# Adaptive max pooling on one core: a small load at the head of the load queue instead of a side load in its middle

## The chip, the core and the metric

The kernel runs on one core of one Trainium2 chip. The metric is the device time of one execution in microseconds (us). The kernel before was run three times: 340.25, 340.25 and 339.33 us, so its median is 340.25 us.

## What is computed

The input `x` is 32 x 256 x 4096 in float32 (134.2 MB). Each row of 4096 values is cut into 256 equal windows of 16 values, and the output holds the maximum of each window (32 x 256 x 256, 8.4 MB).

```python
for i in range(output_size):                 # 256
    start = int(i * length / output_size)    # 16 * i
    end = int((i + 1) * length / output_size)
    result[:, :, i] = np.max(x[:, :, start:end], axis=-1)
```

All windows are alike and lie one after the other in memory, so the kernel sees one long list of 2,097,152 windows of 64 bytes each and may cut it as it likes.

## The kernel before

**The cut.** The list of windows is cut into three spans that follow each other in memory. The first is the *side* span: 16 partitions with 384 windows each (24 KB a partition, L35). The remaining 2,091,008 windows are spread over 128 partitions, 16,336 to a partition, in two groups (L37): group 0 has 7,600 windows a partition, group 1 has 8,736. Within a group a partition owns one contiguous run of memory (486,400 bytes in group 0, 559,104 bytes in group 1).

**The loads.** A group is loaded in pieces of `CHUNK` = 760 windows: 128 partitions x 47.5 KB, 6,080 KB in all. I call such a piece a full load. Group 0 gives 10 of them, group 1 gives 11 and a last piece of 376 windows (23.5 KB a partition). `load` (L73 to L76) takes the next slot of the ring, issues one DMA from SyncE (the profile's SP queue) and has VectorE (DVE) reduce the slot with one `reduce_max` (L67) into an output tile that stays in SBUF.

**The ring.** `ring` (L41) has three slots of 128 x 47.5 KB, taken in turn by a counter `n_loads`. A load can be issued only when the reduce of the load three places before it has freed its slot. All DMAs, loads and stores, are issued by SP in the order in which the program has them, and a DMA whose slot isn't free holds up all that stand behind it on SP.

**The side load.** When `n_loads` is 11, that is after 10 loads of group 0 and one of group 1, `load_side` (L81 to L89) takes one slot of the ring and issues two DMAs: one for 15 partitions of 24 KB (L84), and one for the last partition (L85), whose row is written as 16 pieces of 1.5 KB. Then one reduce over 16 partitions goes into the tile `side`.

**The stores.** They stand behind all loads on SP, in this order: group 0 (128 x 30,400 bytes), the side tile (16 x 1,536 bytes, put second by L104), the first 7,600 windows of group 1 (128 x 30,400 bytes), and the last 1,136 windows of group 1 (128 x 4,544 bytes). Each waits for the reduces that fill what it stores.

Of the kernel before, what the change touches and what calls it, by code (L numbers as in the profile page):

```python
# [1 line left out]

# [4 lines left out]


@with_exitstack
def kernel(  # L10
    ctx: ExitStack,
    tc: tile.TileContext,
    x: bass.AP,
    output_size: bass.AP,
    out: bass.AP,
):

    nc = tc.nc
    P = nc.NUM_PARTITIONS
    fp32 = mybir.dt.float32

    B, C, L = x.shape
    O = int(output_size)
    assert L % O == 0, (L, O)
    W = L // O
    total = B * C * O  # L30

    SLOTS = 3
    CHUNK = 760

    SIDE_P, SIDE, SIDE_AT = 16, 384, 11  # L35
    rest = (total - SIDE_P * SIDE) // P
    GROUPS = [10 * CHUNK, rest - 10 * CHUNK]  # L37
    CUT = 10 * CHUNK

    pool = ctx.enter_context(tc.tile_pool(name="pool", bufs=1))  # L40
    ring = pool.tile([P, SLOTS, CHUNK * W], fp32, tag="ring", name="ring")  # L41

    xw = x.flatten_outer_dims().rearrange("r (o w) -> (r o) w", w=W)
    ow = out.flatten_outer_dims().rearrange("r o -> (r o)")

    taken = 0

    def group(parts, n):

        nonlocal taken  # L50
        span = slice(taken, taken + parts * n)
        taken += parts * n
        return (
            xw[span].rearrange("(p n) w -> p (n w)", p=parts),
            ow[span].rearrange("(p n) -> p n", p=parts),
        )

    n_loads = 0

    def next_slot(parts, n):  # L60
        nonlocal n_loads
        slot = ring[0:parts, n_loads % SLOTS, 0 : n * W]
        n_loads += 1
        return slot

    def pooled(dst, src):
        nc.vector.reduce_max(  # L67
            out=dst,
            in_=src.rearrange("p (n w) -> p n w", w=W),
            axis=mybir.AxisListType.X,  # L70
        )

    def load(dst, src, a, b):  # L73
        slot = next_slot(P, b - a)
        nc.sync.dma_start(out=slot, in_=src[:, a * W : b * W])  # L75
        pooled(dst[:, a:b], slot)  # L76

    xs, os_ = group(SIDE_P, SIDE)
    side_out = pool.tile([SIDE_P, SIDE], fp32, tag="side", name="side")

    def load_side():  # L81
        slot = next_slot(SIDE_P, SIDE)
        last = SIDE_P - 1
        nc.sync.dma_start(out=slot[0:last], in_=xs[0:last])  # L84
        nc.sync.dma_start(  # L85
            out=slot[last:SIDE_P].rearrange("p (k n) -> p k n", k=16),
            in_=xs[last:SIDE_P].rearrange("p (k n) -> p k n", k=16),
        )
        pooled(side_out, slot)  # L89

    stores = []
    for g, n in enumerate(GROUPS):
        xg, og = group(P, n)
        o = pool.tile([P, n], fp32, tag=f"out{g}", name=f"out{g}")
        for a in range(0, n, CHUNK):
            if n_loads == SIDE_AT:
                load_side()
            load(o, xg, a, min(a + CHUNK, n))
        for a, b in ((0, CUT), (CUT, n)):
            if a < b:  # L100
                stores.append((og[:, a:b], o[:, a:b]))
    assert taken == total

    stores.insert(1, (os_, side_out))  # L104
    for dst, src in stores:
        nc.sync.dma_start(out=dst, in_=src)


# [1 line left out]
_INS = ['x', 'output_size']  # L110
_OUTS = [((32, 256, 256), 'float32')]

_NUMBERS = {'output_size': 256}


# [26 lines left out]
```

## Time and profile before

| what | us |
|---|---|
| median of three runs | 340.25 |
| the profiled execution's own time | 340.25 |
| span of the profiled execution | 338.48 |
| around the span (340.25 - 338.48) | 1.77 |
| first load issued by SP | 0.73 |
| first reduce starts (first full load has landed) | 17.87 |
| one reduce of a full load (128 x 760 windows) | 12.82 |
| last reduce (128 x 376 windows) starts and ends | 323.65, 330.06 |
| DVE busy in all | 281.9 |

In the profile's tables an instruction is named by its line in the kernel, its engine, and the tiles that it writes and reads: `out<-ring` is a reduce, `ring<-in_x_dram` a load, `out_dram<-out` a store. DVE is VectorE, and SPq is the time of SyncE's queue of instructions, here the issue of DMAs. "DMA share" is the mean busy share of the core's 16 DMA engines; it can go over 1 where packets overlap. The trace also holds each DMA packet with its start, its duration and its size. A packet is the run of bytes of one partition, so a full load has 128 packets of 48,640 bytes, 8 to each DMA engine. The core's clock was granted in full (1.00).

### The profile page before, as it was taken

Reading aid. Unit: us, or ns where it says so; the run is one execution under the profiler, and the core shown is the slowest. Engines: PE = TensorE matmul, PEld = TensorE weight load, DVE = VectorE, ACT = ScalarE, POOL = GpSimd, SP = SyncE. Lnnn points to the kernel's source line nnn. Section 1 sums busy time; section 2 is a strip of 40 time slices with the busy share of each in tenths; the row PEclk is TensorE's granted clock in tenths of the full one; section 3 lists DMA queues with packets and bytes.
Section 4 is the critical chain, followed back from the end, with each engine's and each line's share of the span. In section 5 each row is a group of like instructions: output and inputs, shape, how many; then the busy total and the mean of one; then the engine's idle time right before and its main releaser. Section 6 shows DMA issues by size and latency. Waiting matters only on the chain.

```text
span 338.5 us, 117 instructions
## 1 busy us (share of the span) xinstructions
DVE 281.9 (83%) x23; POOL 0.2 (0%) x4
## 2 busy tenths in 40 slices
DVE  0088989889898898989799998989889898898990
POOL 0000000000000000000000000000000000000000
DMA  9999999999999999999999999999999999999995
GB/s 356 414 425 460 437 391 460 454 408 425 460 437 391 460 448 402 437 460 397 288 448 408 431 454 431 408 454 448 402 437 454 431 408 448 454 397 423 441 420 245
DMA packets 3664, 142.61 MB, mean 421 GB/s; under 512 B 432, under 2 KB 448, under 8 KB 576
## 3 DMA queue, kind: packets, MB, share of 16 engines
q1 hardware_dynamic: 3664, 142.61, 98.7%
HBM read 134.22 MB, written 8.39 MB: 421 GB/s over the span
## 4 chain that ended last, share of the span: by engine, by line
DMA 63%; DVE 30%; issue 3%; DVEq 2%; SPq 0%
DMA ring<-in_x_dram 63%; DVE out L67 28%; DVE side L67 2%; DVEq L137 2%; SPq L75 0%
## 5 line engine op out<-in xcount | busy, mean ns | idle before, releaser
L67 DVE TENSOR_REDUCE out<-ring 128x760 f32<-128x12160 f32 (+1 forms) x22 | 275.5, 12528 | 48.1 <-DMA ring<-in_x_dram 48.1
L67 DVE TENSOR_REDUCE side<-ring 16x384 f32<-16x6144 f32 x1 | 6.5, 6529 | 0.0
L123 POOL MEMSET const-uint8-127<- 128x1 uint8 x1 | 0.1, 103 | 0.0
L123 POOL MEMSET const-bfloat16-1.0<- 128x1 bf16 x1 | 0.1, 102 | 0.0
L123 POOL MEMSET const-float32-1.0<- 128x1 f32 x1 | 0.1, 99 | 0.0
L123 POOL MEMSET const-float32-0.0<- 128x1 f32 x1 | 0.1, 98 | 0.2 <-issue 0.2
## 6 DMA issues: line engine op xcount, KB each, us to landing
ring<-in_x_dram SPq DMA_DIRECT2D x21, 6080.0 KB, 30.3
out_dram<-out SPq DMA_DIRECT2D x2, 3800.0 KB, 29.3
ring<-in_x_dram SPq DMA_DIRECT2D x1, 3008.0 KB, 23.1
out_dram<-out SPq DMA_DIRECT2D x1, 568.0 KB, 7.5
ring<-in_x_dram SPq DMA_DIRECT2D x1, 360.0 KB, 20.3
ring<-in_x_dram SPq DMA_DIRECT2D x1, 24.0 KB
out_dram<-side SPq DMA_DIRECT2D x1, 24.0 KB, 31.4
```

Of the source, the lines that this page charges most:

```text
L67: nc.vector.reduce_max(out=dst, in_=src.rearrange("p (n w) -> p n w", w=W), axis=mybir.AxisListType.X,)
L123: nc = _bacc.Bacc("TRN2", target_bir_lowering=False, num_devices=1)
L137: with _tile.TileContext(nc) as tc:
```

## The change

The side span in the middle goes away. In its place the first span of the list is 16 partitions with 128 windows each (8 KB a partition, 128 KB in all). It is loaded by one DMA ahead of all others, takes the first slot of the ring and is reduced first. Its store takes the side store's place. The remaining windows are spread over 128 partitions as before, now 16,368 to a partition: group 0 is unchanged in size, group 1 has 8,768 windows a partition (561,152 bytes), so that its last piece has 408 windows (25.5 KB a partition), and the last store has 128 x 4,672 bytes. Everything else is as it was.

```diff
-    SIDE_P, SIDE, SIDE_AT = 16, 384, 11
-    rest = (total - SIDE_P * SIDE) // P
+    FIRST_P, FIRST = 16, 128
+    rest = (total - FIRST_P * FIRST) // P
     GROUPS = [10 * CHUNK, rest - 10 * CHUNK]
     CUT = 10 * CHUNK
...
-    xs, os_ = group(SIDE_P, SIDE)
-    side_out = pool.tile([SIDE_P, SIDE], fp32, tag="side", name="side")
-
-    def load_side():
-        slot = next_slot(SIDE_P, SIDE)
-        last = SIDE_P - 1
-        nc.sync.dma_start(out=slot[0:last], in_=xs[0:last])
-        nc.sync.dma_start(
-            out=slot[last:SIDE_P].rearrange("p (k n) -> p k n", k=16),
-            in_=xs[last:SIDE_P].rearrange("p (k n) -> p k n", k=16),
-        )
-        pooled(side_out, slot)
+    xf, of = group(FIRST_P, FIRST)
+    first_out = pool.tile([FIRST_P, FIRST], fp32, tag="first", name="first")
+    slot = next_slot(FIRST_P, FIRST)
+    nc.sync.dma_start(out=slot, in_=xf)
+    pooled(first_out, slot)
...
         for a in range(0, n, CHUNK):
-            if n_loads == SIDE_AT:
-                load_side()
             load(o, xg, a, min(a + CHUNK, n))
...
-    stores.insert(1, (os_, side_out))
+    stores.insert(1, (of, first_out))
```

## The prediction

> **What bounds the kernel now.** I read the page's slices first (its second part), then SP's waits, then the timeline around the side load, then windows of equal length.
>
> ```profile
> DVE  0088989889898898989799998989889898898990
> ...
> DMA  9999999999999999999999999999999999999995
> GB/s 356 414 425 460 437 391 460 454 408 425 460 437 391 460 448 402 437 460 397 288 448 408 431 454 431 408 454 448 402 437 454 431 408 448 454 397 423 441 420 245
> ```
>
> Each column is 8.46 us. DMA is at nine tenths or more in all slices but the last, while DVE has gaps everywhere: the stream of DMA bytes sets the time. The bytes a slice jump about because a packet counts where it starts, but one slice stands out: the twentieth (161 to 169 us) moved 288 GB/s although its engines count as busy. That is where the side load runs.
>
> ```profile
> SPq L137 <- DMA out_dram<-out: 7.1, 1, 7.1
> ```
>
> This line of SP's waits shows that the end also belongs to the DMAs: after issuing the last store SP waits 7.1 us for it to land. The last store is issued at 330.01 us, but its packets begin only at 333.24 us and later, each right behind its engine's packets of the store before. So the end is the end of the byte stream, not the last reduce.
>
> ```profile
> 132.91 12.82 DVE L67 TENSOR_REDUCE out<-ring 128x760 f32<-128x12160 f32 x1 [1.57 <-DMA ring<-in_x_dram]
> 145.75 0.40 SPq L84 DMA_DIRECT2D ring<-in_x_dram  x1
> 146.21 0.23 SPq L85 DMA_DIRECT2D ring<-in_x_dram  x1
> 147.28 12.82 DVE L67 TENSOR_REDUCE out<-ring 128x760 f32<-128x12160 f32 x1 [1.56 <-DMA ring<-in_x_dram]
> 160.13 135.08 SPq L75 DMA_DIRECT2D ring<-in_x_dram  x11
> 163.29 12.82 DVE L67 TENSOR_REDUCE out<-ring 128x760 f32<-128x12160 f32 x1 [3.19 <-DMA ring<-in_x_dram]
> 176.03 6.53 DVE L67 TENSOR_REDUCE side<-ring 16x384 f32<-16x6144 f32 x1
> 182.49 12.80 DVE L67 TENSOR_REDUCE out<-ring 128x760 f32<-128x12160 f32 x1
> 195.73 12.82 DVE L67 TENSOR_REDUCE out<-ring 128x760 f32<-128x12160 f32 x1 [0.45 <-DMA ring<-in_x_dram]
> 210.12 12.82 DVE L67 TENSOR_REDUCE out<-ring 128x760 f32<-128x12160 f32 x1 [1.57 <-DMA ring<-in_x_dram]
> ```
>
> A reduce that waited for a DMA starts when its load lands, so these starts are a clock of the stream. Full loads land 14.37 or 14.38 us apart (132.91 to 147.28, 195.73 to 210.12 and everywhere else). Between 147.28 and 195.73 three full loads and the side load landed: 48.45 us against 3 x 14.38 = 43.14. **The side load costs 5.31 us of the stream.** Its bytes would be cheap: 24 KB per engine at the rate of a full load (8 x 47.5 KB in 14.38 us) are 0.91 us. And nothing gives the 5.31 us back: DVE's two late reduces (176.03, 182.49) are caught up by 195.73, where DVE waits for a load again, but the loads stay late to the end.
>
> ```profile
> 60.00:74.39 14.38, 12.82 (x1) 0.00 (x0) 1.00 1.00 433
> ...
> 160.00:166.00 6.00, 2.81 (x2) 0.00 (x0) 1.00 0.96 195
> ```
>
> The columns are the window, its length, DVE and POOL busy, clock, DMA share and GB/s. Both windows have the DMA engines busy, yet the second moves 195 GB/s instead of 433. The packet records show how: a 48,640-byte packet takes 1.796 us everywhere else, and the last load's 24,064-byte packets have a median of 0.895 us; the side's sixteen 24,576-byte packets take 1.95 to 3.24 us (median 2.64, 2.95 times the other), and packets of the next full load up to 4.59 us. Fifteen engines write sixteen neighbouring partitions here, where a full load writes all 128. The records also show that the last partition, written in the code as 16 pieces, went as one 24,576-byte packet, so one engine carried two and one carried none.
>
> The Trainium skill (SBUF — State Buffer, section "Door 1: The DMA port swizzle") would explain it: partitions 0 to 15 reach only 4 of 16 ports, about 109 GB/s. By that the side's 393,216 bytes would need 3.6 us, an estimate; the trace's 5.31 us is more, and it decides.
>
> **The change, part by part.** The sum is made against the profiled execution, 340.25 us (span 338.48 and 1.77 around it); the median of the three runs is the same, one run of them 0.9 us lower.
>
> *Removed: the side load.* Two DMAs, two issues (0.40 + 0.23 us on SP, beside 14 us of queued loads) and a 6.53 us reduce on DVE, covered by DVE's 1.57 us of idle time per load. It also held one of three ring slots with little in it: the next full load was issued at 160.13, when the load ahead had 0.35 to 1.5 us left on the engines. All of this is in the 5.31 us, measured to the last engine. **-5.31 us.**
>
> *Added: bytes of the full stream.* 16,368 - 16,336 = 32 more windows per partition, all in the last load (376 to 408). A full load has 760 in 14.38 us: 14.38 x 32 / 760 = **+0.61 us**. On DVE the last reduce grows from 6.41 us to 6.41 x 408 / 376 = 6.95. That is hidden: the last store is issued 3.23 us before its first packet can follow the store ahead (330.01 to 333.24), and the two stores ahead move back by the same 0.61. An issue takes 1.02 us to its first packet at the head (0.73 to 1.75) and 1.97 us at worst around the side load (160.13 to 162.10), so at least 1.2 us of cover remain; without cover it would cost 0.54.
>
> *Moved: stores.* The total is the same, 8.39 MB. The small store goes from 16 x 1,536 to 16 x 512 bytes; the last store gains 128 bytes a partition, 1,024 bytes per engine, just what the small one loses. The side store landed 0.18 us after the store before it, so 0 to -0.18 us; I take 0. Issues stay at one each, behind the loads.
>
> *Added: the load at the head.* No row shows such a load at the head, so I bound it. The chain in order of time begins so:
>
> ```profile
> 0.73 0.38 SPq L75
> 1.11 0.06 issue
> 1.17 31.04 DMA ring<-in_x_dram
> ```
>
> The second issue starts at 1.17, 0.44 us after the first. The first full load is now second, so its descriptors come 0.44 us later: that is the lower row. Below it only one thing can pull: the first 16 packets took 2.53 us (median) instead of 1.80, a start-up that the small packets could take on themselves while the full load's descriptors are still made; with all of it gained the bound is 0.44 - 0.73 = -0.29. From above the nearest row is the side load itself, scaled by bytes: 5.31 / 3 = 1.77 us. The far end is the whole 5.31. For the value I take the packet row: an 8 KB packet alone would need 0.895 x 8,192 / 24,064 = 0.30 us, times the 2.95 of the side's packets 0.90 us. **+0.90 us.**
>
> Behind that instruction nothing new waits long. The small load holds slot 0, so the third full load is issued after the small reduce. A reduce of 128 windows is some 6.53 / 3 = 2.2 us, done at about 6 to 7 us; two full loads are then queued to about 32 us. If that cover failed the stream would stop, but 25 us are left.
>
> One rule speaks against the change. The row: full loads land 14.38 us apart, and 8 packets of 1.793 us from start to start make 14.34, so one DMA more costs 0.04 us in a full queue. The Trainium skill (DMA: Bandwidth & Descriptors, "Anatomy of one DMA") gives each DMA about 2.0 us fixed besides its bytes at 436 GB/s, measured on another issuing path; that would make 2.3 us of the head load, an estimate, and 337.9 us in all.
>
> Sum: -5.31 + 0.61 + 0.00 + 0.90 = -3.80 us, **336.45 us**.
>
> **Rivals.**
>
> *The collision is dear per event, not per byte (partial).* In the middle, packets of the neighbouring loads were slowed too (4.59 us against 1.80), which need not shrink with 8 KB. At the head there is only one neighbour, after it. Half the middle's cost, 2.66 us: -5.31 + 0.61 + 2.66 = -2.04, 338.2 us.
>
> *The same collision in full, the other side.* At the head, in the first 8 us, the first full load collides with the small one as in the middle, for the whole 5.31 us, and its descriptors come 0.44 us late besides: -5.31 + 0.61 + 5.31 + 0.44 = +1.05, 341.3 us. It decides the sign from a head cost of 4.70 us up, and shows as slower from 5.7. For it: the loss in the middle was 4.4 us beyond the bytes. Against: the collision has a third of the bytes, no load before it to slow, no engine with two packets, and SP has the next loads queued at once.
>
> *It doesn't spread.* If the 128 KB went over one engine, as the last partition did against its code, that engine would be 14.38 / 8 x 131,072 / 48,640 = 4.84 us late: -5.31 + 0.61 + 4.84 = +0.14, 340.4 us. Against: the side store's 16 partitions are 16 packets in the trace, the 15 partitions of the side load 15.
>
> *New pitch.* Partitions of group 1 lie 561,152 instead of 559,104 bytes apart. The trace has two pitches (486,400 in group 0) and 14.38 us in both, so I cost it at nothing.
>
> **How the numbers follow.** A measurement of this kernel can tell about 0.3% (1.0 us) from no change: faster is under 339.2, slower over 341.3. My forecast (a head cost of -0.29 to 1.77 us) has 0.75; half the collision 0.15, still faster; no spreading, or a cost near 4.4 us, 0.07, the same; the full collision 0.03, slower. So faster 0.90, same 0.07, slower 0.03. The forecast's own range is 340.25 - 4.70 - 0.29 = 335.26 to 340.25 - 4.70 + 1.77 = 337.3; to leave no more than 2 in 10 out I reach to the half collision, 338.2.
>
> **What would show it.** Reduces from the second full load to the last that start 14.38 us apart without the gap of 3.19; no slice at 288 GB/s; the first full reduce at 17.87 + 0.9 = 18.8 us (17.6 to 19.6); the last full load's reduce at 18.8 + 20 x 14.38 = 306.4 against 310.83; the last reduce at 6.95 us. It would be wrong if the first full reduce came after 20.5 us, if the full loads' steps were not 14.38 in group 1, or if one engine's packets trailed the others.

## The result

The changed kernel takes 335.88 us (median of 6 runs, 335.73 to 336.04), the kernel before beside it 340.04 us (median of 6): a ratio of 0.9878, 95% interval 0.9864 to 0.9892. It is 1.2% faster, as forecast: 336.45 us was predicted, 335.2 to 338.2 as the range. The profiled execution took 335.84 us, its span is 334.1 us.

The slices of the profile after (DMA share, then GB/s):

```profile
DMA  7998998999999999999989989999999999899997
GB/s 295 466 460 379 466 454 384 466 448 390 466 448 390 466 419 419 466 390 448 466 373 466 454 384 466 448 390 466 437 402 466 414 425 466 379 460 421 435 431 305
```

A slice is now 8.35 us. The hole at 288 GB/s is gone; what is left of 373 to 390 comes back every third slice or so, with neighbours at 466, and is packets counted where they start. Only the first and the last slice are thin. The windows of the same length say it better (window, length, DVE, POOL, clock, DMA share, GB/s):

```profile
60.00:74.39 14.39, 12.82 (x1) 0.00 (x0) 1.00 1.00 433
160.00:174.39 14.39, 12.83 (x2) 0.00 (x0) 1.00 1.00 433
```

The stretch where the side load was moves 433 GB/s like any other. The timeline after, its head, its middle and its end:

```profile
0.73 0.39 SPq L81 DMA_DIRECT2D ring<-in_x_dram  x1
...
3.66 2.27 DVE L67 TENSOR_REDUCE first<-ring 16x128 f32<-16x2048 f32 x1 [3.66 <-DMA ring<-in_x_dram]
18.28 12.82 DVE L67 TENSOR_REDUCE out<-ring 128x760 f32<-128x12160 f32 x1 [12.34 <-DMA ring<-in_x_dram]
32.66 12.82 DVE L67 TENSOR_REDUCE out<-ring 128x760 f32<-128x12160 f32 x1 [1.56 <-DMA ring<-in_x_dram]
...
162.09 12.82 DVE L67 TENSOR_REDUCE out<-ring 128x760 f32<-128x12160 f32 x1 [1.56 <-DMA ring<-in_x_dram]
176.47 12.82 DVE L67 TENSOR_REDUCE out<-ring 128x760 f32<-128x12160 f32 x1 [1.56 <-DMA ring<-in_x_dram]
...
305.90 19.68 DVE L67 TENSOR_REDUCE out<-ring 128x760 f32<-128x12160 f32 x2 [1.55 <-DMA ring<-in_x_dram]
```

The small load is issued first and reduced from 3.66 to 5.93 us. The first full load's reduce starts at 18.28 instead of 17.87: 0.41 us for the head load. From there to the end every full load comes 14.38 us after the other, with 1.56 us of idle time before each reduce, and the last one is at 305.90 instead of 310.83: 4.93 us earlier. The line 305.90 holds two reduces, 12.82 and 6.86 us.

### The profile page after: what moved, and what is told of

The parts are those of the page before. It is cut to its first block, busy times and chain, and to the rows that moved or that the text cites. A ratio compares the mean times of both kernels' runs of the same rounds, so it can differ in the third digit from the quotient of the medians.

```text
span 334.1 us, 115 instructions
## 1 busy us (share of the span) xinstructions
DVE 278.4 (83%) x23; POOL 0.2 (0%) x4
## 4 chain that ended last, share of the span: by engine, by line
DMA 68%; DVE 28%; DVEq 2%; issue 0%
DMA ring<-in_x_dram 68%; DVE out L67 27%; DVEq L128 2%; DVE first L67 1%
## 5 line engine op out<-in xcount | busy, mean ns | idle before, releaser
L67 DVE TENSOR_REDUCE first<-ring 16x128 f32<-16x2048 f32 x1 | 2.3, 2274 | 3.7 <-DMA ring<-in_x_dram 3.7
```

Of the source, the lines that this page charges most:

```text
L67: nc.vector.reduce_max(out=dst, in_=src.rearrange("p (n w) -> p n w", w=W), axis=mybir.AxisListType.X,)
```

## The experiments

All costs are read the same way: the landings (of the last engine) of the full loads on both sides of the small load, in the trace's records, less 14.38 us for each full load between them. For the kernel before this gives 5.31 us again (147.26 to 195.71, three full loads). For a load at the head it is the landing of the first full load, less 17.82 us, the mean of that landing in the eleven profiled executions with nothing at the head. Those eleven scatter from 17.56 to 18.00, so a cost at the head is good to some 0.2 us, one in the middle is read to a few hundredths. But each cost comes from one execution, and with 16 neighbouring partitions in the middle the executions of one kernel differ: 338.66 to 340.61 us with one DMA, 338.74 to 339.78 without a slot. Differences of some tenths between such kernels are therefore not told by the costs. Each run was also timed beside the kernel before on the same chip. The kernel before had a median of 340.38 us beside the three runs with a slot in the middle and the side load at the head, 340.20 beside the three runs without a slot on 16 neighbouring and on 128 partitions and the one without a small load, and 340.21 beside the last four (32, 64 and spread partitions, head load over 128).

| run | partitions | KB | place | own ring slot | cost, us | time, us |
|---|---|---|---|---|---|---|
| before | 15 + 1 | 384 | middle | yes | 5.31 | 340.04 |
| one DMA | 16 | 384 | middle | yes | 4.80 | 339.56 |
| 128 partitions | 128 | 384 | middle | yes | 3.55 | 338.29 |
| small in the middle | 16 | 128 | middle | yes | 3.83 | 339.97 |
| no slot | 16 | 384 | middle | no | 4.60 | 339.28 |
| no slot, spread | 16, every eighth | 384 | middle | no | 2.36 | 337.08 |
| no slot | 32 | 384 | middle | no | 2.38 | 337.06 |
| no slot | 64 | 384 | middle | no | 2.62 | 337.29 |
| no slot | 128 | 384 | middle | no | 0.92 | 335.86 |
| no slot, small | 16 | 128 | middle | no | 1.38 | 337.10 |
| side at the head | 16 | 384 | head | yes | 2.51 | 337.47 |
| changed kernel | 16 | 128 | head | yes | 0.43 | 335.88 |
| head, 128 partitions | 128 | 128 | head | yes | 0.70 | 336.15 |
| no small load | - | - | - | - | - | 335.90 |

My theory P was that the price is crowding: many DMA engines writing few partitions. Its rivals: U, the uneven 15 + 1 cut; S, the ring slot filled with few bytes; H, that the head is cheap and the middle dear, whatever the load.

**One DMA instead of 15 + 1.**

```diff
-        last = SIDE_P - 1
-        nc.sync.dma_start(out=slot[0:last], in_=xs[0:last])
-        nc.sync.dma_start(
-            out=slot[last:SIDE_P].rearrange("p (k n) -> p k n", k=16),
-            in_=xs[last:SIDE_P].rearrange("p (k n) -> p k n", k=16),
-        )
+        nc.sync.dma_start(out=slot, in_=xs)
```

> The kernel before with the side load issued as one DMA over all 16 partitions instead of 15 + 1. Cost of the side load is read as the landings from the full load two places ahead of it to the second behind it, less 3 x 14.38 us; before it was 5.31 us. Theory P (the price is the crowding of many DMA engines on few partitions): the crowding stays, only the one engine with two packets goes; before, that engine trailed the mean of the 16 by 1.7 us, so the cost falls to 3.7 to 4.3 us and the time to 338.6 to 339.2. Rival U (the uneven cut over the engines is the price): cost about 0.9 us, the time of the bytes alone, and 335.8 us. Rival S (the ring slot taken with few bytes lets the queue run thin): unchanged, 5.3 us and 340.2.

Measured: 4.80 us, ratio to before 0.998 (0.9967 to 0.9993). U falls as the main cause: the uneven cut is worth 0.51 us between the two profiles and 0.82 between the medians of the times (340.38 to 339.56), and the interval leaves 0.2 to 1.1. P's 3.7 to 4.3 lies below the 4.80 of this profile; the scatter of this kernel doesn't rule it out.

**384 KB over 128 partitions, with a slot** (on the kernel with one DMA).

```diff
-    SIDE_P, SIDE, SIDE_AT = 16, 384, 11
+    SIDE_P, SIDE, SIDE_AT = 128, 48, 11
```

> The kernel before with the side load's same 384 KB spread over 128 partitions (48 windows, 3 KB each), one DMA, in the same place and with its own ring slot. Theory P: without the crowding it costs its bytes, 0.9 us, plus at most some tenths: 0.9 to 1.4 us, and 335.8 to 336.4 in all. Rival U: the same 0.9, since the cut is even. Rival S: the slot is still taken with 0.9 us of bytes, and the next full load is issued as late as before: 4.5 to 5.3 us, 339.4 to 340.2.

Measured: 3.55 us, ratio 0.9943 (0.9926 to 0.9959). No theory had this: without crowding 2.6 us are lost beyond the bytes. Its timeline:

```profile
145.58 0.33 SPq L83 DMA_DIRECT2D ring<-in_x_dram  x1
147.11 12.82 DVE L67 TENSOR_REDUCE out<-ring 128x760 f32<-128x12160 f32 x1 [1.56 <-DMA ring<-in_x_dram]
159.96 47.02 SPq L75 DMA_DIRECT2D ring<-in_x_dram  x5
161.50 12.82 DVE L67 TENSOR_REDUCE out<-ring 128x760 f32<-128x12160 f32 x1 [1.57 <-DMA ring<-in_x_dram]
174.23 0.94 DVE L67 TENSOR_REDUCE side<-ring 128x48 f32<-128x768 f32 x1
179.36 12.82 DVE L67 TENSOR_REDUCE out<-ring 128x760 f32<-128x12160 f32 x1 [4.18 <-DMA ring<-in_x_dram]
```

The side load itself lands at 162.43, 0.95 us after the full load ahead. It is the full load behind it that is late: 179.36. That load was issued at 159.96, when its slot came free, with only 1.5 us of a full load and the side's 0.9 us left in the queue; usually a full load stands between. The packet records show the engines' first packets of it starting from 161.42 to 163.66, up to 3.70 us after the issue, though the last engine had ended the side load by 162.0: four engines got nothing before 162.62 to 163.66. Many of these and the next packets take 2.1 to 2.75 us instead of 1.80. So S is a price too: this load, issued so shortly before the queue ran dry, came late to some engines.

**The small load in the middle, with a slot** (one DMA, `SIDE_P, SIDE, SIDE_AT = 16, 128, 11`).

> The load of 16 x 8 KB of the changed kernel, put where the side load was (after 11 full loads) instead of at the head. At the head it cost 0.41 us. Theory P, price by bytes: a third of the side load, 1.2 to 1.8 us here, since in a full stream nothing hides it; 336.6 to 337.3 in all. Rival H (the collision is dear per event in a running stream, and only the head is cheap): 3 to 5.3 us, 338.4 to 340.8. Rival S: the slot is held with only 0.3 us of bytes, so the queue runs still thinner: 5.3 us or more, 340.8 or more.

Measured: 3.83 us, ratio 0.9988 (0.9979 to 0.9998): moved from the middle to the head, the very load of the changed kernel falls from 3.83 to 0.4 us. The price of 16 x 8 KB is thus mostly where it stands. The timeline says which part:

```profile
160.09 30.53 SPq L75 DMA_DIRECT2D ring<-in_x_dram  x4
162.40 12.82 DVE L67 TENSOR_REDUCE out<-ring 128x760 f32<-128x12160 f32 x1 [2.34 <-DMA ring<-in_x_dram]
175.13 2.26 DVE L67 TENSOR_REDUCE side<-ring 16x128 f32<-16x2048 f32 x1
177.44 12.82 DVE L67 TENSOR_REDUCE out<-ring 128x760 f32<-128x12160 f32 x1
194.21 12.82 DVE L67 TENSOR_REDUCE out<-ring 128x760 f32<-128x12160 f32 x1 [3.95 <-DMA ring<-in_x_dram]
```

The load behind the small one lands at 177.42; it is the next that comes 16.77 us after it. That one was issued at 175.25, 0.8 to 1.9 us before the engines ran out (their last packets of the load ahead ended from 176.04 to 177.11); its last engine started at 178.80, 3.55 us after the issue.

A queue that runs dry isn't enough, though. The load behind the small one was issued as late, at 160.09, when the engines had 0.65 to 2.14 us of packets left. It reached every engine within 2.14 us, the engines' idle time before it was 3 us in all, against 11 before the load that was late, and the two steps up to its landing (15.16 and 15.05 us) hold 1.45 us in all, about what this small load costs without a slot (1.38, below). Why one late load comes late to its engines and the other not stays open. Besides, the last load of this run lands 8.22 us after the load ahead, where its bytes give 7.72; that half microsecond is in the run's time and not in its cost.

**The side load at the head** (one DMA, `SIDE_AT = 0`).

> The side load of 16 x 24 KB in one DMA at the head of the queue. Theory P, price by bytes: what the head hid of the small load (1.2 to 1.8 less 0.41, about 1.1 us) it hides here too, so 3.7 to 4.3 less 1.1: 2.6 to 3.2 us, and the first full load's reduce at 20.5 to 21.1 us; 337.5 to 338.1 in all. Rival H (the head is cheap whatever the bytes): 0.41 plus the bytes of 16 KB more per engine, 0.6: 1.0 us, first full reduce at 18.9 and 335.9 in all.

Measured: the first full load landed at 20.33 (its reduce starts at 20.35), so 2.51 us; ratio 0.9915 (0.9901 to 0.993). H falls: with 24 KB the head is not cheap. P's 2.6 to 3.2 is missed by little. It is still about half of the 4.80 in the middle, and at the head the price doesn't follow the bytes: 0.43 us for 8 KB, 2.51 for 24 KB.

**Without a ring slot.** The next runs put the side load into the space of group 1's output tile, which nothing uses yet, behind the ninth full load. So crowding stands alone. (The output tiles are made ahead of the loop for this; those lines are left out here.)

```diff
-        slot = next_slot(SIDE_P, SIDE)
+        slot = outs[1][0:SIDE_P, 0 : SIDE * W]
         nc.sync.dma_start(out=slot, in_=xs)
...
-    SIDE_P, SIDE, SIDE_AT = 16, 384, 11
+    SIDE_P, SIDE, SIDE_AT = 16, 384, 9
```

> The side load of 16 x 24 KB in one DMA in the middle of the stream, but into the still unused space of group 1's output tile, issued right behind the ninth full load: no ring slot is taken, and over 14 us of loads stand ahead of every issue. With its own ring slot it cost 4.80 us. Theory max (crowding and a late refill of the queue lie beside each other in the middle, and crowding is the longer here): the refill goes, the crowding stays, 3.6 to 4.8 us; 338.6 to 339.8 in all. Rival sum (the two add up): 4.80 less the 2.64 us that the 128-partition form lost beyond its bytes: 2.2 us and 337.2. Rival S (the slot alone is the price): 0.9 us and 335.9.

Measured: 4.60 us, ratio 0.9969 (0.9956 to 0.9982). Taking no slot helps the crowded load by 0.20 us only (0.10 between the medians of the times, each against its kernel before), and that can't be told from no help at all: crowding and late refill lie beside each other there, and crowding is the longer. The packets of the run with a slot show it. Its load behind the side load was issued at 160.30, and no engine stood idle before it: their side packets kept all sixteen busy until 1.94 to 5.43 us after the issue.

> The same 384 KB over 128 partitions (3 KB each), in the middle, without a ring slot: neither crowding nor a thin queue. With its own slot it cost 3.55 us. Both the max and the sum theory: its bytes, 0.9 to 1.0 us, and 335.9 in all. If it still costs 2 us or more, there is a price for a small load in the middle that neither crowding nor the slot explains.

(`SIDE_P, SIDE, SIDE_AT = 128, 48, 9`.) Measured: 0.92 us, the time of the bytes alone; ratio 0.9865 (0.985 to 0.9879). With a slot the same load cost 3.55. Its timeline, in which the side load lands between the loads of the two full reduces:

```profile
132.62 12.82 DVE L67 TENSOR_REDUCE out<-ring 128x760 f32<-128x12160 f32 x1 [1.55 <-DMA ring<-in_x_dram]
145.35 0.94 DVE L67 TENSOR_REDUCE side<-out 128x48 f32<-128x768 f32 x1
147.93 12.82 DVE L67 TENSOR_REDUCE out<-ring 128x760 f32<-128x12160 f32 x1 [1.63 <-DMA ring<-in_x_dram]
```

The two kernels also differ in the place (behind 9 or 11 full loads) and in the space written; that the late issue makes the difference is read from the packet records above.

> The load of 16 x 8 KB in the middle without a ring slot; with a slot it cost 3.83 us, at the head 0.41. If crowding is paid by bytes: a third of what the 24 KB form costs without a slot, 1.2 to 1.6 us, 336.2 to 336.6 in all; then most of the 3.83 was the late refill. If crowding is dear per event: 3 us or more, 338 or more.

(`SIDE_P, SIDE, SIDE_AT = 16, 128, 9`.) Measured: 1.38 us, ratio 0.9903 (0.9888 to 0.9918). That is nearly a third of 4.60: in the middle crowding is paid by bytes. The other 2.45 of the 3.83 us with a slot are the late load shown there.

**Which partitions.**

> The 384 KB of the side load over 32 neighbouring partitions (12 KB each), in the middle, without a ring slot. Over 16 partitions it cost 4.60 us, over 128 partitions 0.92. If crowding falls with the number of partitions: half of 4.60, 2.3 us. If it is a fixed price of any load under 128 partitions: 4 us or more. The Trainium skill (SBUF - State Buffer, Door 1: The DMA port swizzle) states eight ports of sixteen for partitions 0 to 31; by its figures this is about 1.8 us, an estimate.

> The same 384 KB over 64 neighbouring partitions (6 KB each), in the middle, without a ring slot. If crowding falls with the number of partitions: a quarter of 4.60, 1.15 us. If it is a matter of which partitions share a way into SBUF, it can stop falling: the same as over 32 partitions. The Trainium skill (SBUF - State Buffer, Door 1: The DMA port swizzle) states that partitions 0 to 63 reach no more ports than 0 to 31; by it this kernel's side load costs what the 32-partition one does, about 1.8 us, an estimate.

(`SIDE_P, SIDE, SIDE_AT = 32, 192, 9` and `64, 96, 9`.) Measured: 2.38 and 2.62 us, ratios 0.9905 (0.9885 to 0.9925) and 0.9911 (0.9892 to 0.9931). Half of 4.60 with 32 partitions, but no further fall with 64, and 0.92 with 128: the number of partitions alone is not it.

**Every eighth partition** (on the kernel without a slot).

```diff
-        slot = outs[1][0:SIDE_P, 0 : SIDE * W]
-        nc.sync.dma_start(out=slot, in_=xs)
+        slot = outs[1][:, 0 : SIDE * W]
+        nc.sync.dma_start(out=slot[0 : P : P // SIDE_P], in_=xs)
...
+    nc.gpsimd.memset(outs[1][:, 0 : SIDE * W], 0.0)
...
-    stores.insert(1, (os_, side_out))
+    stores.insert(1, (os_, side_out[0 : P : P // SIDE_P]))
```

> The side load of 16 x 24 KB in the middle without a ring slot, but into every eighth partition (0, 8, ..., 120) instead of 0 to 15: as many packets, as long, as many engines. Its reduce runs over all 128 partitions (the others hold zeros) and its store takes every eighth. On 0 to 15 it cost 4.60 us. If the few partitions alone are the price (16 is 16): 4.6 us again and 339.3 in all. If neighbouring partitions share a way into SBUF: clearly less, about half, 1.9 to 2.6 us and 336.8 to 337.5. The Trainium skill (SBUF - State Buffer, Door 1: The DMA port swizzle) puts these sixteen on eight ports and the neighbouring sixteen on four; by it about 1.8 us, an estimate.

Measured: 2.36 us, ratio 0.9903 (0.9886 to 0.992), with the same sixteen packets. The windows around it, first of the kernel with neighbouring partitions, then of this one:

```profile
132.00:138.00 6.00, 2.78 (x1) 0.00 (x0) 1.00 0.91 247
```

```profile
132.00:138.00 6.00, 4.40 (x1) 0.00 (x0) 1.00 1.02 369
```

The same side load between the same full loads, in the same 6 us: 247 GB/s against 369. Sixteen neighbours cost 4.60 us, sixteen that are spread 2.36: neighbouring partitions share a way in. The packets agree: median 3.01 us against 1.62 (0.90 for the last load's packets of nearly this size, 24,064 bytes, over all partitions).

The Trainium skill (SBUF — State Buffer, "Door 1: The DMA port swizzle") has this map: four ports for partitions 0 to 15, eight for 0 to 31, for 0 to 63 and, by its formula, for the spread sixteen, sixteen for all 128. The order of the five costs is that map's. By its rates the five would cost 3.6, 1.8 (three times) and 0.9 us, estimates; measured were 4.60, 2.36 to 2.62 and 0.92, so for the crowded loads the rates are too kind here.

**The head load over 128 partitions** (`FIRST_P, FIRST = 128, 16` in the changed kernel).

> The small load at the head with the same 128 KB over 128 partitions (1 KB each) instead of 16. In the changed kernel it cost 0.41 us: its own 0.30 of bytes is in that, or the second issue that comes 0.44 us later, or crowding. If the later issue or the bytes are the price: again 0.3 to 0.5 us, first full reduce at about 18.2 and 335.9 in all. If crowding is: 0.0 to 0.1 us, first full reduce at 17.8 to 17.9 and 335.5.

Measured: 0.70 us and 336.15; ratio 0.9877 (0.9862 to 0.9892). The first lines of its timeline:

```profile
1.15 30.57 SPq L75 DMA_DIRECT2D ring<-in_x_dram  x4
...
18.54 12.82 DVE L67 TENSOR_REDUCE out<-ring 128x760 f32<-128x12160 f32 x1 [15.28 <-DMA ring<-in_x_dram]
```

Taking the crowding away from the head load gains nothing. What both head loads share is a second issue some 0.4 us later (1.15 and 1.18 against 0.73). So no crowding shows in the price of 8 KB at the head; that the price is the later issue fits in size, within the scatter of 0.2 us, and no run shows it alone.

**No small load at all** (in the changed kernel, the small load, its reduce and its store taken out, 16,384 windows a partition).

> No small load at all: 16,384 windows per partition over 128 partitions, the last load 424 windows. Against the changed kernel 0.41 us go (the head load) and 16 windows more per partition come, 0.30 us: 335.7 to 335.9 against its 335.9, no difference that can be told. If the small load at the head does something for the stream that isn't seen yet (the engines' start in step, for one), this kernel is slower: 336.5 or more.

Measured: 335.90 us, ratio 0.9868 (0.9852 to 0.9885). The small load at the head is neither a gain nor a loss that can be told; what the change brings is that the side load is gone from the middle. No run beat the changed kernel by more than can be told.

## Why the prediction was right, point by point

- **What bounds.** Right: the stream of DMA bytes. SP still waits 7.1 us for the last store's landing in the profile after:

```profile
SPq L128 <- DMA out_dram<-out: 7.1, 1, 7.1
```

- **Removed, -5.31 us.** Right in size, and mostly in cause. The profiles split it: 4.60 is crowding (0.92 of that the bytes), 0.51 the uneven 15 + 1 cut, and 0.20 the ring slot, which I named but did not price. The two small parts lie within the scatter of these kernels (the medians of the times give 0.82 and 0.10). The slot is cheap only under the crowding: in the run with 128 partitions, where nothing covers it, 2.6 us go with it.
- **More bytes in the stream, +0.61 us.** The last load landed 7.76 us after the load ahead, 7.13 before: +0.63. The last reduce took 6.86 us, 6.95 was expected, and was hidden: the last store was issued 5.04 us before its first packet (325.60, 330.64). The prediction's cover had a weak spot. Its 1.97 us from an issue to the first packet "at worst" is the earliest of one load's sixteen engines, and the last engine's came up to 3.70 us after the issue in the run with 128 partitions and a slot.
- **Stores, 0.** The four stores landed 9.07, 0.18, 8.80 and 1.45 us one after the other, 9.06, 0.18, 8.87 and 1.42 before: -0.03.
- **The head load, +0.90 us.** The term that was mis-sized: 0.41 us between the two profiles (0.43 against the mean). I took the slowdown of the side's packets, 2.95 times, for the small packets. They took 0.51 us (median), 1.7 times the 0.30 alone, and the 1.38 us that the same load costs in the middle without a slot did not come through at the head. The lower row, the second issue 0.44 us later, comes nearest: the first full load's first packets started at 2.27 to 3.55 us on the sixteen engines, 1.75 to 3.09 before, so 0.5 us later. But several engines went straight from their small packet to it, so the later issue and the small packets can't be told apart here. The start-up that could have pulled the cost under 0.44 was not absorbed: the full load's first packets still took 2.39 us (median), 2.53 before.
- **Sum.** -5.31 + 0.61 + 0.90 = -3.80 predicted; -5.31 + 0.41 + 0.63 - 0.03 = -4.30 from the parts, -4.34 in the landing of the last store (337.48 to 333.14), -4.41 in the profiled executions' times (340.25 to 335.84) and -4.16 in the medians (340.04 to 335.88).
- **Rivals.** The collision dear per event, in part or in full, falls: at the head the small load cost 0.4 us against 2.66 and 5.31, and in the middle 8 KB cost 1.38 us and 24 KB cost 4.60 without a slot, nearly 1 to 3 as the bytes. "It doesn't spread" falls: the small load is 16 packets of 8,192 bytes, which started within 0.18 us of each other. The new pitch costs nothing: the loads of group 1 land 14.37 to 14.39 us apart too.
- **The rule that speaks against it.** The Trainium skill (DMA: Bandwidth & Descriptors, "Anatomy of one DMA"), with a figure measured on another issuing path, would charge the head load 2.3 us, an estimate. The head load cost 0.4, and 384 KB over 128 partitions in a full queue cost their bytes, 0.92 us. In the full queue of these runs its fixed part of about 2 us does not show; where the queue ran dry a loss of that size came up twice (2.63 and 2.45 us), and once it did not.

## What to carry to other kernels

In a kernel bound by its DMA stream, measure a small load by the landings on both sides of it, not by its bytes: 0.9 us of bytes cost 5.3 here. Cut remainders over all 128 partitions, and if a few partitions must do, spread them; look also at what the ring has queued when the next load is issued, since a ring slot with few bytes in it can stall a load after it. Over 16 neighbouring partitions the small load was cheaper at the head (0.43 us) than in the middle without a slot (1.38); over all 128 partitions, without a slot, a load in the middle cost its bytes alone; and leaving the small load out cost nothing that can be told.

## What the runs showed that I had not expected

- Sixty-four neighbouring partitions took a load no faster than 32 (2.62 and 2.38 us for 384 KB), and 16 spread ones as fast as 32 neighbours (2.36).
- A full load that is issued with 0.7 to 2.1 us of packets left on the engines can cost about 2.5 us: in two runs the last engine's first packet started 3.55 and 3.70 us after the issue, and the next packets were long too. In a third case, as late, it started within 2.14 us and no such cost showed. The same 384 KB over 128 partitions cost 3.55 us with a ring slot and 0.92 without.
- A row written as 16 pieces of 1.5 KB in the code went as one packet of 24,576 bytes, so that one engine had two packets and one none; that was worth 0.51 us between two profiles, 0.82 between medians, and more than nothing by the interval of the times.
